# A scan's diagonal blocks moved by GpSimd, and its scale put on the keys

## Chip, cores and metric

The kernel runs on one core of a Trainium2 chip. The metric is the device time of one execution in microseconds. A profile of one execution stands beside the times: it names the engines PE (TensorE matmuls), PEld (TensorE weight loads), DVE (VectorE), ACT (ScalarE), POOL (GpSimd) and SP (SyncE), and writes a q behind the name where only the engine's queue is meant, as in ACTq for a DMA that ScalarE begins.

## The reference

One encoder layer on a 1024 x 1024 input: a normalization, one wide projection, two token mixers (a convolution module, and a bidirectional gated scan with 8 heads of 128), a gated merge, an output product, and a feed-forward block. All in float32. The part that matters here is the scan:

```python
qh = heads(jax.nn.silu(q) * (HGRN_HEAD_DIM ** -0.5))
lf_f, k_f = _forget_log_and_key(z_fwd, lb_fwd)    # f = lb + (1-lb) sigmoid(z)
lf_b, k_b = _forget_log_and_key(z_bwd, lb_bwd)    # key = (1-lb) sigmoid(-z)
o_fwd = _chunk_gated_scan(qh, heads(k_f), vh, heads(lf_f))
o_bwd = flip(_chunk_gated_scan(flip(qh), flip(heads(k_b)), flip(vh), flip(heads(lf_b))))
# S_t = diag(f_t) S_{t-1} + k_t v_t^T,  o_t = S_t^T q_t
...
```

So the key of each direction carries a factor per channel, `1 - lb`, and the query a constant, `128 ** -0.5`. Their product `kscale` (one column per head and direction) may be put on either side of the score `q k`.

## The kernel before

The projection, the merge and the feed-forward block are long rows of float32 products, each split into three products of rounded parts (`mm3`, lines 148 to 150). The scan is woven into the end of the projection. It goes head by head, and each head in two halves of 512 positions, so 16 scans `i`, each with a chain of its own:

- `scan_inputs(i)` loads `q` and the two gates' inputs, and ScalarE makes from each input the key's sigmoid into `kG` (line 1162), the gate's sigmoid (1163) and the forget gate `f` (1164); VectorE clips `f` (1165). `kG` has both directions side by side, 2 x 512 columns, as have `f` and `qF`.
- `scan_base` builds the scores inside blocks of 32 positions by doubling: at each size `h` a copy of the keys and of the queries is woven together on ScalarE (`woven`, line 1175, tiles `A`), VectorE multiplies half of `kG` and of `qF` by the totals of the forget gates (`double_keys`, `double_queries`, `totals`, all shown at line 1143), and TensorE makes small products (`level`, 1194). The result is gathered by masks into `D_t`, 128 x 4 x 32 (lines 1260 and 1262).
- `scan_levels` goes on to 64 and 128, with TensorE making the larger blocks (`blocks`, 1284). ScalarE copies them to `S_t` (1312), 128 x 4 x 128, and four DMAs put the four diagonal blocks of `D_t` into `S_t` (1314), 32 partitions and 16 KB each.
- `scan_states` turns the keys on TensorE (1324), copies them on ScalarE (`kT`, 1326) and forms the states (1333).
- `outputs`, one head later, multiplies `S_t`, `qF` and the states with values (1374), copies the result (`tm`, 1376), squares it (1379), takes the norm on GpSimd (`ors`, 591 and 592), and scales (1393).

The loop over heads and halves runs `scan_levels` and `scan_states` of scan `i`; `between(n)` after each piece puts in some TensorE work of the projection (`dense.fill(FILL)`), one step of the previous head's `outputs`, and one step of `scan_base` of the scans `i + 1` (`ahead`) or `i + 2` (`following`).

TensorE's order is the order in which the program writes its instructions:

```python
ctx.enter_context(tc.manual_schedule(engines={mybir.EngineType.PE}))
```

The other engines' orders are made by a planner from the dependences, a cost model and the order of writing; each engine then runs its queue strictly in that order. Tiles have a fixed number of buffers (8 for `A`, 3 for `kG`, `D` and `S`, 4 for `qF`), and a new one waits until the readers of the oldest are done.

`nc.scalar`, also called `A`, is ScalarE; `V` is VectorE, `G` GpSimd, `T` TensorE. `tt` is a VectorE product of two tensors, `view(t, off, dims)` an access pattern by offset and steps, and `pairs(t, h)` the pattern that takes, in the two directions, every second block of `h` columns.

Of the kernel before, what the change touches and what calls it, by code (L numbers as in the profile page):

```python
# [15 lines left out]
ALU = mybir.AluOpType  # L16
# [15 lines left out]
H = 512  # L32
# [5 lines left out]
def view(t, off, dims):  # L38

    return bass.AP(  # L40
        tensor=t.tensor,
        offset=t.offset + off,
        ap=[list(t.ap[0])] + [list(d) for d in dims],
    )
# [3 lines left out]
def tile_hybrid_encoder(  # L48
# [22 lines left out]
    nc = tc.nc  # L71
    PSUM = bass.MemoryType.PSUM
    V, A, G, T = nc.vector, nc.scalar, nc.gpsimd, nc.tensor
# [20 lines left out]
    def nm(s):  # L94
        uid[0] += 1
        return f"{s}_{uid[0]}"
# [3 lines left out]
    def bank(tag):  # L100
        return ps.tile([P, H], F32, tag=tag, name=nm(tag), bufs=BANKS[tag])

    def page(pool, tag, bufs, dt=F32):
        return pool.tile([P, H], dt, tag=tag, name=nm(tag), bufs=bufs)
# [10 lines left out]
    def load(src):  # L115
        t = tmp()
        nc.sync.dma_start(t, src)
        return t
# [670 lines left out]
    for j in range(NCW):  # L789
        g = gp0.tile([P, PAD + S + PAD], F32, tag="gl", name=nm("gl"), bufs=NCW)  # L790
# [341 lines left out]
    for k in range(NK2):  # L1132
        t = load(d_h[k][1])
# [8 lines left out]
    def tt(o, a, b, op=ALU.mult):  # L1142
        V.tensor_tensor(o, a, b, op=op)  # L1143
# [4 lines left out]
    def c4(t):  # L1148
        return t.rearrange("p (c t) -> p c t", c=4)
# [18 lines left out]
    def pairs(t, h, other=H):  # L1168

        return view(t, 0, [[other + h, 2], [2 * h, H // (2 * h)], [1, h]])  # L1170

    def woven(t, h):

        t_h = page(hp, "A", 8)
        A.copy(pairs(t_h, h, 0), pairs(t, h))  # L1175
        return t_h

    def slot(b, n):
        return b[:, n * P : (n + 1) * P]

    def near(t):
        return t.rearrange("p (c t) -> p c t", c=4)

    def over(m):
        return view(m, 0, [[0, 4], [1, 32]])

    def each():
        for c in range(4):
            for g in range(0, P, 32):
                yield c * P + g, slice(g, g + 32), slice(32 * c, 32 * c + 32)  # L1190

    def level(b, A_t, Q_t):
        for at, g, o in each():
            T.matmul(b[g, o], A_t[:, at : at + 32], Q_t(at), start=True, stop=True)

    def row(t):
        return lambda at: t[:, at : at + 32]

    def double_keys(kG, tb, h):
        n, nb = H // (2 * h), H // h  # L1200
        tt(pairs(kG, h), pairs(kG, h), view(tb, 1, [[nb - 1, 2], [2, n], [0, h]]))

    def double_queries(qF, q, tb, h):
        n, nb = H // (2 * h), H // h
        tt(pairs(qF, h), q, view(tb, nb + 1, [[-(nb + 1), 2], [2, n], [0, h]]))

    def totals(tb, h, to=None):
        n, nb = H // (2 * h), H // h
        tn = None
        if to is None:  # L1210
            tn = hp.tile([P, 2, n], F32, tag=f"tb{h}", name=nm("tb"), bufs=1 if h < 8 else 2)
            to = view(tn, 0, [[n, 2], [1, n]])
        tt(to, view(tb, 0, [[nb, 2], [2, n]]), view(tb, 1, [[nb, 2], [2, n]]))
        return tn

    def scan_base(ins):


        q, f, kG, ks = ins
        qF = hp.tile([P, 2, H], F32, tag="qF", name=nm("qF"), bufs=4)  # L1220
        D_t = hp.tile([P, 4, 32], F32, tag="D", name=nm("D"), bufs=3)
        k_d, Q1 = page(hp, "A", 8), page(hp, "A", 8)
        V.tensor_scalar(k_d, kG[:, 1, :], ks[:, 1:2], None, op0=ALU.mult)
        V.scalar_tensor_tensor(k_d, kG[:, 0, :], ks[:, 0:1], k_d, op0=ALU.mult, op1=ALU.add)
        A1 = woven(kG, 1)
        odd = H // 2

        def gated(to, at, t, d):
            V.scalar_tensor_tensor(
                view(to, at, [[2, odd]]),  # L1230
                view(q, t, [[2, odd]]),
                ks[:, d : d + 1],
                view(f, d * H + t, [[2, odd]]),
                op0=ALU.mult,
                op1=ALU.mult,
            )

        for t in range(2):
            gated(Q1, t, t, 1 - t)
        for t in (1, 0):  # L1240
            gated(qF, (1 - t) * H + t, t, t)
        double_keys(kG, f, 1)
        double_queries(qF, pairs(Q1, 1, 0), f, 1)
        tb = totals(f, 1)
        yield
        A2, Q2 = woven(kG, 2), woven(qF, 2)
        double_keys(kG, tb, 2)
        double_queries(qF, pairs(qF, 2), tb, 2)
        tb = totals(tb, 2)
        A4, Q4 = woven(kG, 4), woven(qF, 4)  # L1250
        yield
        b = bank("sc")
        for n, (k_t, q_t) in enumerate(((k_d, q), (A1, Q1), (A2, Q2), (A4, Q4))):
            level(slot(b, n), k_t, row(q_t))
        double_keys(kG, tb, 4)
        double_queries(qF, pairs(qF, 4), tb, 4)
        tb = totals(tb, 4)
        A8, Q8 = woven(kG, 8), woven(qF, 8)
        yield
        A.copy(D_t, near(slot(b, 3)))  # L1260
        for n, m in enumerate((m_d, m_1, m_2)):
            V.copy_predicated(D_t, over(m), near(slot(b, n)))
        double_keys(kG, tb, 8)
        double_queries(qF, pairs(qF, 8), tb, 8)
        tb = totals(tb, 8)
        A16, Q16 = woven(kG, 16), woven(qF, 16)
        yield
        double_keys(kG, tb, 16)
        double_queries(qF, pairs(qF, 16), tb, 16)
        tb = totals(tb, 16)  # L1270
        yield qF, kG, tb, D_t, A8, Q8, A16, Q16

    def scan_levels(base, S_t, Tt):


        qF, kG, tb, D_t, A8, Q8, A16, Q16 = base

        def blocks(b, h):

            for c in range(0, H, P):  # L1280
                for s0 in range(0, P, h):
                    t0 = s0 ^ h
                    d = s0 // h % 2
                    T.matmul(
                        b[s0 : s0 + h, c + t0 : c + t0 + h],
                        kG[:, d, c + s0 : c + s0 + h],
                        qF[:, 1 - d, c + t0 : c + t0 + h],
                        start=True,
                        stop=True,
                    )  # L1290

        def double(tb, h, to=None):
            double_keys(kG, tb, h)
            double_queries(qF, pairs(qF, h), tb, h)
            return totals(tb, h, to)

        b = bank("ob")
        level(slot(b, 0), A8, row(Q8))
        level(slot(b, 1), A16, row(Q16))
        S_b = bank("sc")  # L1300
        for at, g, _ in each():
            T.matmul(S_b[g, at : at + 32], none, none, start=True, stop=True)
        blocks(S_b, 32)
        for n, m in enumerate((m_8, m_16)):
            V.copy_predicated(D_t, over(m), near(slot(b, n)))
        tb = double(tb, 32)
        yield
        yield
        b = S_b
        blocks(b, 64)  # L1310
        double(tb, 64, view(Tt, 0, [[4, 2], [1, 4]]))
        A.copy(S_t, c4(b))
        for g in range(0, P, 32):
            nc.scalar.dma_start(S_t[g : g + 32, :, g : g + 32], D_t[g : g + 32])
        yield

    def scan_states(i, kG, v, Tt, Sf, Sb):
# [91 lines left out]
    class Base:  # L1409
        def __init__(self, ins):  # L1410
            self.gen, self.val = scan_base(ins), None
# [40 lines left out]
    for h in range(NH):  # L1452
# [4 lines left out]
        for half in range(2):  # L1457
# [11 lines left out]
            S_t = hp.tile([P, 4, P], F32, tag="S", name=nm("S"), bufs=3)  # L1469
# [9 lines left out]
            qF, kG = base[:2]  # L1479
# [499 lines left out]
    for s in range(SEVENS):  # L1979
        todo = [(FIRST + 2 * NS * s, i, k) for i in PRODUCTS for k in range(NS)]  # L1980
        if s == 0:
            at = [12 + 2 * n for n in range(12)] + [starts[0] - 8 + n // 2 for n in range(6)]
            at += [starts[0] - 5 + n for n in range(3)]
        else:
            at = [starts[s] - 36 + 6 * n for n in range(NS)]
# [59 lines left out]
```

## Time and profile before

| | before |
|---|---|
| median of 3 runs | 1735.89 us (1734.44 to 1736.55) |
| the profiled execution | 1732.47 us |
| its span, first to last instruction | 1730.7 us |
| mean granted TensorE clock | 0.998 |
| DMAs begun by GpSimd (software queue) | 44800 packets, 37.76 MB |
| DMAs begun by ScalarE (queue 10) | 9216 packets, 1.05 MB |

Engine times are shares of the span. A busy TensorE is not one at its peak, but TensorE idle is time in which nothing was multiplied. The idle time of an engine ends with what released it; where the text before `<-` is an engine and line, that is the one that waited. In the windows' rows the last columns are the granted TensorE clock as a share of full speed, the mean busy share of the DMA engines and GB/s. The queue of ScalarE carries only the 64 transfers of line 1314; all others are begun by SyncE or GpSimd.

### The profile page before, as it was taken

Reading aid. Unit: us, or ns where it says so; the run is one execution under the profiler, and the core shown is the slowest. Engines: PE = TensorE matmul, PEld = TensorE weight load, DVE = VectorE, ACT = ScalarE, POOL = GpSimd, SP = SyncE. Lnnn points to the kernel's source line nnn. Section 1 sums busy time; section 2 is a strip of 40 time slices with the busy share of each in tenths; the row PEclk is TensorE's granted clock in tenths of the full one; section 3 lists DMA queues with packets and bytes.
Section 4 is the critical chain, followed back from the end, with each engine's and each line's share of the span. In section 5 each row is a group of like instructions: output and inputs, shape, how many; then the busy total and the mean of one; then the engine's idle time right before and its main releaser. Section 6 shows DMA issues by size and latency. Waiting matters only on the chain. (4 is left out here: it accounts for less than half of the span.)

```text
span 1730.7 us, 30713 instructions
## 1 busy us (share of the span) xinstructions
PE 1702.4 (98%) x11902; PEld 1415.8 (82%) x11902; DVE 1257.2 (73%) x1953; ACT 824.4 (48%) x1544; POOL 170.6 (10%) x185
## 2 busy tenths in 40 slices
PE   8999999999999999999999999999999999999997
PEld 6878887888788888888888888888888888888787
DVE  4599999746778888878657466767776877657864
ACT  7444433334566777776442245444434443542334
POOL 2211111100000000000000002011111111000110
PEclk9999999999999999999999999999999999999999
DMA  8768887855673434435579466577777877783842
GB/s 285 241 170 187 197 193 187 210 160 156 207 226 102 133 127 133 127 115 186 176 249 331 153 205 206 145 155 149 174 172 156 183 170 162 231 263 102 213 93 98
DMA packets 343752, 308.28 MB, mean 178 GB/s; under 512 B 25262, under 2 KB 255798, under 8 KB 343606
## 3 DMA queue, kind: packets, MB, share of 16 engines
q1 hardware_dynamic: 289590, 267.51, 48.7%
q0 software_dynamic: 44800, 37.76, 15.2%
q10 hardware_dynamic: 9216, 1.05, 0.4%
q8 instruction: 93, 1.52, 0.3%
q14 instruction: 53, 0.43, 0.1%
HBM read 201.40 MB, written 87.03 MB: 167 GB/s over the span
## 5 line engine op out<-in xcount | busy, mean ns | idle before, releaser
L148 PE MATMUL mm<-hx,wp 128*128 128x512 f32 x1068 | 427.3, 400 | 2.7 <-ACT tm L850 1.5
L150 PE MATMUL mm<-hx,wp 128*128 128x512 f32 x1068 | 417.5, 391 | 1.2 <-DVE wp L124 1.2
L149 PE MATMUL mm<-hx,wp 128*128 128x512 f32 x1068 | 416.6, 390 | 0.0
L124 ACT CAST wp<-wr 128x1024 fp32r<-128x1024 f32 (+2 forms) x147 | 147.3, 1002 | 254.3 <-PE mm L149 111.0
L150 PEld LDWEIGHTS mm<-hx,wp 128*128 128x128 f32 x1068 | 200.6, 188 | 46.2 <-DVE wp L124 3.4
L148 PEld LDWEIGHTS mm<-hx,wp 128*128 128x128 f32 x1068 | 200.9, 188 | 45.4 <-DVE ev L799 2.2
L149 PEld LDWEIGHTS mm<-hx,wp 128*128 128x128 f32 x1068 | 201.0, 188 | 39.8 <-issue 1.0
L124 DVE TENSOR_TENSOR wp<-wr,wp 128x1024 fp32r<-128x1024 f32 (+2 forms) x145 | 169.5, 1170 | 71.2 <-ACT wp L124 64.8
L1038 DVE SCALAR_TENSOR_TENSOR acc<-gl,v_b,acc 128x1024 f32<-128x1024 f32 x120 | 149.1, 1279 | 0.4
L439 ACT COPY su<-mm 128x512 f32<-128x512 f32 x82 | 47.7, 581 | 56.9 <-PE mm L150 56.3
L1143 DVE TENSOR_TENSOR qF<-qF,tb 128x512 f32<-128x512 f32 x96 | 65.7, 686 | 6.9 <-ACT A L1175 6.7
L148 PE MATMUL tr<-hx,wp 128*128 128x512 f32 x180 | 70.5, 392 | 0.0
L124 ACT CAST wq<-sw 128x1024 fp32r<-128x1024 f32 x41 | 43.2, 1054 | 56.8 <-PE mm L149 46.2
L150 PE MATMUL tr<-hx,wp 128*128 128x512 f32 x180 | 70.1, 389 | 0.0
L149 PE MATMUL tr<-hx,wp 128*128 128x512 f32 x180 | 70.0, 389 | 0.0
L1641 DVE SCALAR_TENSOR_TENSOR tm<-gp,v_a,tm 128x512 f32<-128x512 f32 x88 | 66.0, 750 | 3.9 <-ACT tm L1639 2.0
L1143 DVE TENSOR_TENSOR kG<-kG,tb 128x512 f32<-128x512 f32 x96 | 65.1, 685 | 0.5 <-ACT A L1175 0.4
L148 PE MATMUL mm<-hy,wp 128*128 128x512 f32 x164 | 64.2, 391 | 0.0
L148 PE MATMUL sc<-hy,wq 128*128 128x512 f32 x164 | 64.2, 391 | 0.0
L150 PE MATMUL sc<-hy,wq 128*128 128x512 f32 x164 | 63.8, 389 | 0.0
L149 PE MATMUL mm<-hy,wp 128*128 128x512 f32 x164 | 63.8, 389 | 0.0
L149 PE MATMUL sc<-hy,wq 128*128 128x512 f32 x164 | 63.8, 389 | 0.0
(372 smaller groups left out, 3616.5 us busy)
## 6 DMA issues: line engine op xcount, KB each, us to landing
wr<-in_w_in_dram SPq DMA_DIRECT2D x48, 512.0 KB, 4.8
wr<-in_ffn_w_up_dram SPq DMA_DIRECT2D x22, 512.0 KB, 4.0
sw<-in_w_in_dram SPq DMA_DIRECT2D x38, 256.0 KB
d_g<-ft SPq DMA_DIRECT2D x38, 256.0 KB, 2.8
sw<-in_ffn_w_up_dram SPq DMA_DIRECT2D x38, 256.0 KB, 4.5
sw<-in_ffn_w_up_dram POOLq DMA_DIRECT2D x19, 512.0 KB, 8.1
wr<-sw POOLq DMA_DIRECT2D x32, 256.0 KB, 3.4
wr<-wr POOLq DMA_DIRECT2D x32, 256.0 KB, 4.0
```

Source lines behind the costliest of these rows:

```text
L124: parts = A.copy(hi, src), eng.tensor_tensor(lo, src, hi.bitcast(F32), op=ALU.subtract)
L148: T.matmul(acc, whi[:, k, :], ahi, start=first, stop=False, skip_group_check=again)
L149: T.matmul(acc, whi[:, k, :], alo, start=False, stop=False, skip_group_check=again)
L150: T.matmul(acc, wlo[:, k, :], ahi, start=False, stop=last, skip_group_check=again)
L439: A.copy(t, acc)
L1038: V.scalar_tensor_tensor(acc, g[:, k : k + S], tap(k), acc, op0=ALU.mult, op1=ALU.add)
L1143: V.tensor_tensor(o, a, b, op=op)
L1641: V.scalar_tensor_tensor(c, g[:, o + k : o + k + H], vec("fdw", k * NF + j), c, op0=ALU.mult, op1=ALU.add,)
```

## The change

Two places in the scan. In `scan_levels` the four DMAs from `D_t` to `S_t` are begun by GpSimd. In `scan_base` both directions of `kG` are multiplied in place by their column of `kscale`; the sum `k_d` of the directions is then a plain addition, and `Q1` and the first half of `qF` are each one product of `q` and `f` with a pattern over both parities, where there were two products with a scalar for each.

```diff
         D_t = hp.tile([P, 4, 32], F32, tag="D", name=nm("D"), bufs=3)
+        for d in range(2):
+            V.tensor_scalar(kG[:, d, :], kG[:, d, :], ks[:, d : d + 1], None, op0=ALU.mult)
         k_d, Q1 = page(hp, "A", 8), page(hp, "A", 8)
-        V.tensor_scalar(k_d, kG[:, 1, :], ks[:, 1:2], None, op0=ALU.mult)
-        V.scalar_tensor_tensor(k_d, kG[:, 0, :], ks[:, 0:1], k_d, op0=ALU.mult, op1=ALU.add)
+        tt(k_d, kG[:, 0, :], kG[:, 1, :], ALU.add)
         A1 = woven(kG, 1)
         odd = H // 2
-
-        def gated(to, at, t, d):
-            V.scalar_tensor_tensor(
-                view(to, at, [[2, odd]]),
-                view(q, t, [[2, odd]]),
-                ks[:, d : d + 1],
-                view(f, d * H + t, [[2, odd]]),
-                op0=ALU.mult,
-                op1=ALU.mult,
-            )
-
-        for t in range(2):
-            gated(Q1, t, t, 1 - t)
-        for t in (1, 0):
-            gated(qF, (1 - t) * H + t, t, t)
+        tt(
+            pairs(Q1, 1, 0),
+            view(q, 0, [[1, 2], [2, odd], [1, 1]]),
+            view(f, H, [[1 - H, 2], [2, odd], [1, 1]]),
+        )
+        tt(
+            view(qF, 1, [[H - 1, 2], [2, odd]]),
+            view(q, 1, [[-1, 2], [2, odd]]),
+            view(f, H + 1, [[-(H + 1), 2], [2, odd]]),
+        )
         double_keys(kG, f, 1)
...
         A.copy(S_t, c4(b))
         for g in range(0, P, 32):
-            nc.scalar.dma_start(S_t[g : g + 32, :, g : g + 32], D_t[g : g + 32])
+            G.dma_start(S_t[g : g + 32, :, g : g + 32], D_t[g : g + 32])
         yield
```

## The prediction

> **What bounds the kernel now.** I read the page first, then the busy time by windows, then the waits and the timeline inside the stage that the change touches.
>
> ```profile
> span 1730.7 us, 30713 instructions
> PE 1702.4 (98%) x11902; PEld 1415.8 (82%) x11902; DVE 1257.2 (73%) x1953; ACT 824.4 (48%) x1544; POOL 170.6 (10%) x185
> 486.00:880.00 394.00, 386.45 (x5966) 329.88 (x5964) 308.33 (x683) 268.02 (x612) 14.69 (x16) 1.00 0.46 145
> 915.00:1600.00 685.00, 685.00 (x3027) 566.61 (x3026) 464.07 (x638) 279.38 (x411) 73.23 (x69) 1.00 0.70 183
> ```
>
> TensorE is busy 98% of the span. The scan stage runs from 486 to 880 us; the first two lines of the windows give it and the later stage: columns are PE, PEld, DVE, ACT, POOL busy, clock, DMA share, GB/s. In the scan TensorE is busy 386.45 of 394.00, so at most 7.55 us can be won there by waiting less, while from 915 to 1600 it is never idle and nothing can be won. TensorE's order is written out by hand, so its work is the same before and after; only its waits can change. These are they, for the scan stage:
>
> ```profile
> PE tr L1324 <- DVE kG L1143: 4.7, 3, 2.2
> PE sc L1333 <- ACT kT L1326: 1.4, 2, 0.7
> PE sc L1194 <- ACT A L1175: 1.3, 2, 1.0
> ```
>
> So TensorE waits for the finished keys (`kG`) before it turns them, for ScalarE's copy of the turned keys (`kT`), and for ScalarE's weaves (`A`). The longest of these waits is followed by a slower clock:
>
> ```profile
> 720.00:724.00 4.00, 1.86 (x9) 1.87 (x10) 4.00 (x7) 0.88 (x2) 0.00 (x0) 0.74 0.84 258
> 724.00:728.00 4.00, 4.00 (x19) 3.33 (x19) 4.00 (x10) 3.83 (x8) 0.00 (x0) 0.83 0.70 217
> 722.14 1.11 PE L1324 MATMUL tr<-ident,kG 128*128 128x128 f32 x4 [2.24 <-DVE kG L1143]
> ```
>
> The missing clock in the two windows is 0.26 x 4 + 0.17 x 4 = 1.7 us. I put it down to the 2.24 us wait just in front of it. [...]
>
> **The four transfers leave ScalarE.**
>
> ```profile
> L1314 ACTq DMA_DIRECT2D S<-D x64: 592/612/1323, 523.1 to 856.5; - x64
> 676.53 2.55 ACTq L1314 DMA_DIRECT2D S<-D  x4
> 679.18 1.05 ACT L124 CAST wp<-wr 128x1024 fp32r<-128x1024 f32 x1 [2.68 <-DMA S<-D]
> 680.13 0.58 ACT L1326 COPY kT<-tr 128x512 f32<-128x512 f32 x1
> 680.76 0.94 PE L1333 MATMUL sc<-v,kT 128*128 128x128 f32 x6 [0.63 <-ACT kT L1326]
> ```
>
> Each of the 16 scans holds ScalarE's queue for about 2.55 us (four issues of 0.612 and their gaps), 16 x 2.55 = 41 us. Idle time "until DMA S<-D" is this issuing. At 676.53 it stands in front of a cast and of `kT`; `kT` ends at 680.71 and TensorE starts at 680.76, after 0.63 us of waiting. With the four issues gone `kT` can be 2.55 us earlier, so both waits of this kind vanish: -1.4.
>
> The other place is further from TensorE:
>
> ```profile
> 697.83 1.92 ACTq L1314 DMA_DIRECT2D S<-D  x3
> 700.88 0.39 PE L1374 MATMUL ob<-Sf,qF 128*128 128x128 f32 x2
> 702.31 0.59 ACT L1376 COPY tm<-ob 128x512 f32<-128x512 f32 x1
> 706.16 0.20 POOL L591 TENSOR_SCALAR ors<-oss 128x8 f32<-128x8 f32 x1 [43.64 <-ACT jk L1379]
> 712.32 0.70 DVE L1165 TENSOR_SCALAR f<-f 128x1024 f32<-128x1024 f32 x1 [2.67 <-ACT f L1164]
> 714.13 0.69 DVE L1143 TENSOR_TENSOR kG<-kG,tb 128x512 f32<-128x512 f32 x1
> 714.73 0.69 DVE L1143 TENSOR_TENSOR qF<-qF,tb 128x512 f32<-128x512 f32 x1
> 715.33 0.48 DVE L1229 SCALAR_TENSOR_TENSOR qF<-q,kscale,f 128x256 f32<-128x256 f32 x1
> 715.73 0.68 DVE L1143 TENSOR_TENSOR kG<-kG,tb 128x512 f32<-128x512 f32 x1
> 721.39 0.69 DVE L1143 TENSOR_TENSOR kG<-kG,tb 128x512 f32<-128x512 f32 x1
> ```
>
> This chain ends in the 2.24 us wait. The transfers keep ScalarE until 699.75, so the copy `tm` of the finished output starts at 702.31 though the matmuls ended at 701.27: 1.04 us late. After it come squares, GpSimd's `ors` at 706.16, the scaling on ScalarE, the forget gate `f`, VectorE's clip at 712.32, and then VectorE without a pause until `kG` is done at 722.08, 0.06 us ahead of TensorE. Without the issues `tm` starts on time and the chain moves by up to 1.04. I take all of it for this wait, and half of what remains of the other waits for `kG` (4.7 - 2.24 = 2.5, half 1.2) and of those for `A` (1.3, half 0.65), as the same chain lies in front of them with smaller lateness.
>
> **What GpSimd pays.**
>
> ```profile
> L301 POOL DMA_DIRECT2D wr<-wr x32: 847/856/866, 128.6 to 1464.2; - x32
> L301 POOL DMA_DIRECT2D sw<-in_w_in_dram x13: 1570/1582/1757, 85.6 to 327.8; - x13
> DMA to landing us min/median/max: 3.2/4.4/9.8
> 854.53 2.56 ACTq L1314 DMA_DIRECT2D S<-D  x4
> 870.46 0.39 PE L1374 MATMUL ob<-v,S 128*128 128x128 f32 x2
> ```
>
> A transfer begun by GpSimd has 0.86 us for the small and 1.58 for the large form (medians). No such transfer of 16 KB is in the trace; I take the small one, 4 x 0.86 = 3.4 us a scan, bounds 3.4 to 6.3. GpSimd is free: 14.69 of 394 us busy. What stands behind the four on its queue is `ors`: at the quoted head they would begin at 697.2 and end by 703.5 at the dear price, ahead of 706.16. Landing takes 3.2 to 9.8 us from issue. The tightest use of a block seen is the last one: begun at 854.53, last issue at 854.5 + 3 x 1.58 = 859.3, landed at 869.1 at worst, used at 870.46. Cost nothing; it is hidden by the 16 us between copy and use, and if that cover were gone it would cost the overshoot, up to some 8 us at one place (a rival below).
>
> **The scaling moves from queries to keys.**
>
> ```profile
> L1223 DVE TENSOR_SCALAR A<-kG,kscale 128x512 f32<-128x512 f32 x16 | 7.7, 480 | 4.9 <-ACT kG L1162 4.9
> L1224 DVE SCALAR_TENSOR_TENSOR A<-kG,kscale,A 128x512 f32<-128x512 f32 x16 | 12.0, 747 | 0.2
> L1229 DVE SCALAR_TENSOR_TENSOR qF<-q,kscale,f 128x256 f32<-128x256 f32 x32 | 14.7, 481 | 3.4 <-PE ob L1374 3.3
> L1229 DVE SCALAR_TENSOR_TENSOR A<-q,kscale,f 128x256 f32<-128x256 f32 x32 | 14.4, 481 | 0.0
> L1143 DVE TENSOR_TENSOR qF<-A,f 128x512 f32<-128x512 f32 x16 | 11.0, 688 | 0.0
> ```
>
> Removed per scan: 480 + 747 + 4 x 481 = 3151 ns. Added: two scalings of 480 and three products of 688 (nearest row: `qF<-A,f`, same size and stride), 3024 ns. By durations VectorE gains 0.13 us a scan, 2 us over 16, not on the path as a sum. What matters is where. Back to back, instructions start closer than they last: 0.60 apart for the product (714.13 to 714.73), 0.40 for the half-size one (715.33 to 715.73). In the unbroken run to 722.08 stand the two half-size `qF` instructions, 0.80 together; one product of 0.60 replaces them: -0.19 on the long wait. The two scalings (0.40 each by the same overlap, an estimate) need only the key's sigmoids, which ScalarE makes before `f`; VectorE idles 2.67 us in front of 712.32, and I place them there, at no cost. If that cover is gone they cost 0.80 a scan. The wait that is added: the first weave of a scan on ScalarE reads `kG` and now waits for both scalings, with the weaves, casts and evacuations of its queue behind it, and VectorE's first `kG` product waits for that weave. Bounds: 0 (the Q1 and qF products, 1.2 us, lie between) and the price of the slower rival. I take 0.
>
> **Sum.** -1.4 (kT) -1.04 -0.19 (long wait) -1.2 -0.65 (other waits) = -4.5; with the long wait at about 1.0 in place of 2.24 the clock stays up, -1.7: -6.2. The profiled execution took 1732.47 us (span 1730.7 and 1.8 around it), 3.4 below the median of the runs, 1735.89, and 2.0 below their lowest, so the difference is carried over: 1735.9 - 6.2 = 1729.7.
>
> **Rivals.**
>
> *Slower: the scaled keys become a link VectorE to ScalarE to VectorE.*
>
> ```profile
> ACT A L1175 <- DVE kG L1143: 17.7, 23, 2.5
> ```
>
> ScalarE's waits for keys cost 17.7 / 23 = 0.77 us each. If the first weave joins them in every scan, and in half of the scans (one of each head, where an unbroken VectorE run ends in the turn of the keys) the delay passes through, TensorE waits 8 x 0.77 = 6.2 more; two more waits that pull the clock down add 3.4; the sure -1.4 stays: +8.2, 1744.1. It decides from 0.06 us, the distance between `kG` and TensorE at 722.08. For it: this slack, and that VectorE, ScalarE and GpSimd are ordered by a planner, so new dependences reshuffle all three. Against it: the idle 2.67.
>
> *No change: the freed queue time is spent waiting.* ScalarE would then wait for the matmuls of `ob` or for GpSimd's `ors`; only the -1.4 remains: 1734.5.
>
> *GpSimd and VectorE hinder each other.* 64 x 0.86 = 55 us of GpSimd issuing is 14% of the stage; of 48 VectorE scalings and clips 6.7 would meet one, at up to 0.86 each: +5.8, which eats the gain: 1735.5. The trace has no such meeting of these shapes. [...]
>
> *The transfers go late.* If the planner puts `ors` in front of the four, or they land at the slow end behind it, the last block misses 870.46 by up to 8 us while only -6.2 is won: about 1738.
>
> **How the numbers follow.** About 0.2%, 3.5 us, is what a measurement of this kernel can tell from no change. Forecast 0.40; no change 0.13 and hindrance 0.06 make "same" 0.19; slower by the link 0.33, late transfers 0.04, another shuffle of the order 0.04 make 0.41. The forecast's own range runs from all waits and the clock (-7.55 - 1.7, 1726.6) to the edge of the bound (1732.4). The whole range reaches from there over no change to the slower rival, 1726.6 to 1744.5, and leaves worse shuffles out.
>
> **What would show it.** Right: no transfer on ScalarE's queue and no wait "until DMA S<-D"; no TensorE wait for `kT`; waits for `kG` near 2 us in sum and full clock at all windows; TensorE idle below 3 us in the scan stage. Wrong: clip or scalings standing at the end of long VectorE idle times, first weaves waiting for the scalings, more or longer waits for `kG`, further windows with clock below 1, transfers of GpSimd far over 1 us each, or TensorE waiting for `S`.

## The result, and the profile after

The changed kernel took 1729.89 us (median of 9 runs, 1728.12 to 1733.97) beside 1734.67 us for the kernel before on the same chip: a ratio of 0.9971 [0.9961, 0.9981], that is 3.3 to 6.8 us less. The forecast was 1729.7.

From the profile's page of the changed kernel (its head and the busy times):

```profile
span 1732.2 us, 30782 instructions
...
PE 1704.5 (98%) x11902; PEld 1416.5 (82%) x11902; DVE 1255.2 (72%) x1937; ACT 826.1 (48%) x1544; POOL 206.5 (12%) x249
```

This profiled execution, 1733.97 us, is the slowest of the nine, and its span is no shorter than the one before. So whole spans can't be subtracted; the stage has to be compared by itself. Two rows of each profile mark it: the first product of the first scan (`sc<-q,A`, first start) and the last product of the outputs (`ob<-v,S`, last start). Before:

```profile
L1194 PE MATMUL sc<-q,A x512: 196/196/218, 503.0 to 831.7; 128*32 128x32 f32 x171
L1374 PE MATMUL ob<-v,S x128: 272/275/275, 558.0 to 872.6; 128*128 128x128 f32 x128
```

After:

```profile
L1194 PE MATMUL sc<-q,A x512: 196/196/218, 504.7 to 825.9; 128*32 128x32 f32 x171
L1370 PE MATMUL ob<-v,S x128: 272/275/275, 559.5 to 866.8; 128*128 128x128 f32 x128
```

The stage took 872.6 - 503.0 = 369.6 before and 866.8 - 504.7 = 362.1 after. 1.7 of the 7.5 is the low clock that lay inside the stage before; about 6 is left. After, the windows' row of the stage (columns as before) with the rows at two low clocks outside it, and then the waits of TensorE and VectorE in the stage:

```profile
486.00:880.00 394.00, 390.16 (x5999) 334.55 (x5998) 311.07 (x671) 271.48 (x618) 50.36 (x80) 1.00 0.47 149
...
96.00:100.00 4.00, 2.11 (x5) 1.72 (x6) 2.31 (x4) 2.16 (x4) 0.00 (x0) 0.69 0.98 313
900.00:904.00 4.00, 2.95 (x9) 1.88 (x10) 3.15 (x6) 1.96 (x4) 0.00 (x0) 0.89 1.07 314
```

```profile
PE tr L1320 <- DVE kG L1143: 3.8, 3, 2.0
...
DVE kG L1223 <- ACT kG L1162: 25.3, 13, 4.6
...
DVE f L1165 <- ACT f L1164: 6.1, 6, 1.4
DVE qF L1143 <- ACT A L1175: 4.6, 7, 2.0
```

Of VectorE's waits before, the prediction did not show these:

```profile
DVE f L1165 <- ACT f L1164: 17.9, 8, 5.5
...
DVE qF L1143 <- ACT A L1175: 6.7, 11, 2.3
```

TensorE is idle for 3.84 us instead of 7.55. Its waits for `kT` and for `A` are gone; those for `kG` are left. VectorE's idle time stands in front of the keys' scalings (L1223), where the prediction put them: 25.3 us there and 6.1 in front of the clip, where it had 17.9. ScalarE has no wait "until DMA S<-D" any more. The timeline at the two places that the prediction followed:

```profile
676.77 0.59 ACT L1308 COPY S<-sc 128x512 f32<-128x512 f32 x1
677.28 1.05 ACT L124 CAST wp<-wr 128x1024 fp32r<-128x1024 f32 x1
...
677.66 2.25 POOL L1310 DMA_DIRECT2D S<-D  x4 [13.42 <-ACT S L1308]
...
678.73 0.58 ACT L1322 COPY kT<-tr 128x512 f32<-128x512 f32 x1
...
709.86 0.49 DVE L1223 TENSOR_SCALAR kG<-kG,kscale 128x512 f32<-128x512 f32 x1 [3.46 <-ACT kG L1162]
...
711.86 0.69 DVE L1165 TENSOR_SCALAR f<-f 128x1024 f32<-128x1024 f32 x1 [0.96 <-ACT f L1164]
...
721.56 0.66 PE L1320 MATMUL tr<-ident,kG 128*128 128x128 f32 x4 [1.38 <-DVE kG L1143]
```

Behind the copy to `S` ScalarE goes straight on to the cast and `kT`, while GpSimd issues the four transfers beside it. One scaling ends a VectorE wait of 3.46 us, and the wait at `kG` is 1.38.

### The profile page after: what moved, and what is told of

The parts are those of the page before. It is cut to its first block, busy times and chain, and to the rows that moved or that the text cites. A ratio compares the mean times of both kernels' runs of the same rounds, so it can differ in the third digit from the quotient of the medians.

```text
span 1732.2 us, 30782 instructions
## 1 busy us (share of the span) xinstructions
PE 1704.5 (98%) x11902; PEld 1416.5 (82%) x11902; DVE 1255.2 (72%) x1937; ACT 826.1 (48%) x1544; POOL 206.5 (12%) x249
## 5 line engine op out<-in xcount | busy, mean ns | idle before, releaser
L1310 POOL DMA_DIRECT2D S<-D x64 | 35.5, 560 | 286.7 <-ACT jk L1375 127.7
L148 PE MATMUL sc<-hy,wq 128*128 128x512 f32 x164 | 64.2, 391 | 0.0
L150 PE MATMUL sc<-hy,wq 128*128 128x512 f32 x164 | 63.8, 389 | 0.0
```

What stands on the lines that cost most here:

```text
L148: T.matmul(acc, whi[:, k, :], ahi, start=first, stop=False, skip_group_check=again)
L150: T.matmul(acc, wlo[:, k, :], ahi, start=False, stop=last, skip_group_check=again)
L1310: G.dma_start(S_t[g : g + 32, :, g : g + 32], D_t[g : g + 32])
```

## The experiments

The theory: ScalarE's queue time was what TensorE waited behind, and the keys' scalings cost nothing, since they stand in VectorE's idle time. The rivals: the scaled keys are a link that delays ScalarE and VectorE; GpSimd's issuing hinders VectorE; the low clock explains the difference; the planner's new order is only a lucky one.

**The transfers alone, to GpSimd.** The kernel before with

```diff
-            nc.scalar.dma_start(S_t[g : g + 32, :, g : g + 32], D_t[g : g + 32])
+            G.dma_start(S_t[g : g + 32, :, g : g + 32], D_t[g : g + 32])
```

> The kernel before with one edit: the four transfers begun by GpSimd; the queries are scaled as before. Theory A (the gain comes from ScalarE's freed queue): 0.6 to 0.85 of the change, -3 to -4.5 us, no TensorE wait for kT, TensorE idle in the scan stage down from 7.55 to about 4. Theory B (the gain comes from VectorE's work moved into its idle times): at most -1.4 us, the two waits for kT. Theory C (the gain is a lucky order of the planner's): anything, with no relation to the sum of the parts.

1732.5 beside 1736.4: 0.998 [0.9968, 0.9992]. TensorE's waits in the stage:

```profile
PE tr L1324 <- DVE kG L1143: 4.4, 5, 1.7
PE sc L1194 <- ACT A L1175: 0.8, 1, 0.8
```

The waits for `kT` are gone with this part alone. A wait of 0.8 for a weave is left, and the waits for `kG` are shorter but more.

**The keys alone.** The change without that line: ScalarE goes on issuing the transfers.

> The kernel before with the other edit: keys scaled twice by VectorE, transfers begun by ScalarE as before. Theory A: -0.2 to -1.2 us (0.19 a run of VectorE, six runs), waits for kT still 1.4 us. Theory B: -3.5 to -5 us. Theory C: anything; e1 and e2 together far from the -5.0 of the whole change.

1738.03 beside 1736.4: 1.0008 [0.9998, 1.0018], no gain. The waits of TensorE and VectorE in the stage:

```profile
PE tr L1320 <- DVE kG L1143: 4.8, 3, 2.2
PE sc L1194 <- ACT A L1175: 1.9, 2, 1.5
PE sc L1329 <- ACT kT L1322: 1.4, 2, 0.9
...
DVE kG L1223 <- ACT kG L1162: 27.0, 14, 4.0
...
DVE qF L1143 <- ACT A L1175: 9.2, 13, 2.3
```

VectorE waits in front of the scalings as in the changed kernel, but waits longer for ScalarE's weaves (9.2 us; 6.7 before, 4.6 after), and TensorE's three kinds of waits are those of before. Its low clock stands behind the wait at 588, not at 722 (windows):

```profile
588.00:592.00 4.00, 3.61 (x14) 3.12 (x15) 4.00 (x10) 1.92 (x5) 0.00 (x0) 0.64 0.65 171
592.00:596.00 4.00, 4.00 (x26) 3.51 (x25) 2.76 (x10) 3.86 (x8) 0.00 (x0) 0.94 0.38 115
```

**The transfers alone, to SyncE.** As the first, with `nc.sync.dma_start`: no GpSimd instruction is added.

> The kernel before with the four transfers begun by SyncE. Theory A (what counts is that they leave ScalarE): as with GpSimd, within 1 us of e1. Rival D (GpSimd's queue was needed, since SyncE's is full of loads behind waits): the transfers hold up the loads of the scans and of the weights behind them, 0 to +5 us against the kernel before, with new waits for loads (q, zi, wr) in the scan stage.

1730.91 beside 1736.4: 0.9967 [0.9956, 0.9979]. Its waits are those of GpSimd's version (`kG` 4.5 in 5, `A` 0.8 in 1), and its stage is 364.6 beside 364.8. So what counts is that ScalarE is left, not who takes over.

**The keys scaled by ScalarE.** The change without VectorE's two scalings; ScalarE makes the key, scale included, as an affine function of the gate's sigmoid:

```diff
             A.activation(kG[:, d, :], z, AF.Sigmoid, scale=-1.0)
...
+            A.activation(
+                kG[:, d, :], z, AF.Identity,
+                scale=knegative[:, ks : ks + 1], bias=kscale[:, ks : ks + 1],
+            )
...
-        for d in range(2):
-            V.tensor_scalar(kG[:, d, :], kG[:, d, :], ks[:, d : d + 1], None, op0=ALU.mult)
```

> The changed kernel with the scaling of the keys done by ScalarE in the gate itself: the key is kscale - kscale x sigmoid(z), one instruction of about 0.82 us in place of a sigmoid of 0.63, and VectorE's 32 scalings of 0.48 are gone. Theory A: VectorE's scalings stood in idle time, so taking them away wins under 0.5 us; ScalarE's longer key instruction (2 x 0.19 a scan) lies in front of the clip and costs up to 0.2 to 0.4 us at each of the waits for kG: 0 to +1.5 us against the changed kernel. Theory E (the link from VectorE's scalings to the first weaves costs time): -1 to -2.5 us against the changed kernel.

1732.05 beside 1736.4: 0.9979 [0.9968, 0.999]. Here there is no link from VectorE's scaling to ScalarE's first weave, and VectorE has the 32 scalings less in the scan. TensorE's waits:

```profile
PE tr L1324 <- DVE kG L1143: 3.0, 4, 1.4
```

The stage is 362.3, that of the changed kernel. The link has no price that shows in the stage. (ScalarE's instruction for the key has the form of the one that makes `f` here, 816 ns beside 632 for the key's sigmoid in the first trace of the kernel before, so that this run by itself could hide a small price; the last experiment doubles the scalings instead.)

**The change with the transfers on SyncE.**

> The changed kernel with the four transfers begun by SyncE in place of GpSimd: scaled keys and a free ScalarE, GpSimd left out. Theory A (it counts that ScalarE is free; then the scaled keys are worth 1.5 to 2.7 us more): 1.0 us about the changed kernel, -5 to -7.5 us against the kernel before, scan stage from first to last of its products about 362 us. Rival D (SyncE's loads are held up when the scan runs faster): slower than the changed kernel by 1 us or more, with new waits for loads. Rival F (GpSimd's issuing hinders VectorE in the changed kernel): faster than the changed kernel by 2 us or more.

1729.65 beside 1736.81: 0.9955 [0.9941, 0.9969]; stage 363.5, of which 1.7 is a low clock from 588.7 on.

**Twice the issues on GpSimd.** The change with eight transfers of 16 partitions in place of four of 32:

```diff
-        for g in range(0, P, 32):
-            G.dma_start(S_t[g : g + 32, :, g : g + 32], D_t[g : g + 32])
+        for g in range(0, P, 16):
+            o = g // 32 * 32
+            G.dma_start(S_t[g : g + 16, :, o : o + 32], D_t[g : g + 16])
```

> The changed kernel with each transfer cut in two, 8 by GpSimd a scan in place of 4: the suspected cost on GpSimd is doubled (2.2 us more a scan at the 0.55 us that one was seen to take). Theory A (hidden in the 14 us and more between copy and use): within 1 us of the changed kernel. Rival F (GpSimd's issuing locks VectorE out): VectorE's scalings and clips beside an issue last longer than 0.50 and 0.70 us, and the time is 1 to 5 us over the changed kernel. Rival G (the norm behind the transfers on GpSimd's queue is late): TensorE waits for kG grow by 1 us or more.

1729.83 beside 1736.81: 0.9956 [0.9942, 0.9971]. The rows of the transfers' line, and that of VectorE's scalings among the instructions on `kG`:

```profile
L1311 POOL DMA_DIRECT2D S<-D x128: 512/512/767, 524.4 to 852.6; - x128
...
DMA to landing us min/median/max: 1.6/2.7/4.8
```

```profile
L1223 DVE TENSOR_SCALAR kG<-kG,kscale x32: 469/486/494, 491.0 to 797.0; 128x512 f32<-128x512 f32 x32
```

The scalings last 469 to 494 ns. Few of them overlap an issue: four here, at 475 to 478 ns, and none in the changed kernel. With the transfers alone, however, nine of the 16 scalings of this size do, at 472 to 480 ns, beside 476 to 487 for the other seven. No scaling is held up for the length of an issue, and the rival of a hindrance falls for them; no clip (L1165) overlaps an issue in these three traces, so clips stay untested. The stage is 362.7: TensorE has one wait of 0.6 us that the change has not, for which the profile names no cause.

**The kernel before again,** one execution, for the spread of its trace.

> The kernel before, unchanged, once more with a profile: how far do the waits and the clock of one profile hold? Theory A of the prediction (the 2.24 us wait at 722 us halves the clock behind it): the same wait and the same low clock behind it. [...]

1735.43 us. The wait that the prediction made answerable for the low clock is there again; the low clock is not. Timeline and windows:

```profile
723.41 0.66 PE L1324 MATMUL tr<-ident,kG 128*128 128x128 f32 x4 [2.22 <-DVE kG L1143]
...
817.04 0.39 PE L150 MATMUL mm<-hx,wp 128*128 128x512 f32 x1
818.53 1.16 PE L1333 MATMUL sc<-v,kT 128*128 128x128 f32 x8 [1.10 <-ACT kT L1326]
```

```profile
96.00:100.00 4.00, 2.85 (x8) 2.28 (x9) 1.90 (x4) 2.20 (x4) 0.15 (x1) 0.71 0.76 238
...
720.00:724.00 4.00, 1.78 (x13) 1.37 (x12) 4.00 (x7) 2.15 (x5) 0.00 (x0) 1.00 0.55 175
724.00:728.00 4.00, 4.00 (x26) 3.49 (x25) 4.00 (x10) 2.56 (x5) 0.00 (x0) 1.00 1.01 298
```

**Both: keys by ScalarE, transfers by SyncE.** VectorE and GpSimd are spared.

> The kernel with the key's scale put in by ScalarE's gate instruction (no scaling on VectorE) and the transfers begun by SyncE. Theory A: as the version with GpSimd and that scaling within 1 us, -3 to -5 us against the kernel before, since VectorE's scalings stood in idle time. Theory E (the link from VectorE's scalings to the first weaves costs time): faster than the version of scaled keys and SyncE by 1 us or more.

1731.74 beside 1736.81: 0.9965 [0.9953, 0.9978]; stage 362.0. Sparing either engine brings nothing beyond the change.

**A product moved to GpSimd.** In front of the waits that are left VectorE runs without a pause, so the changed kernel (transfers on SyncE) was tried with the projection's weight subtraction (`wp`, 1.22 us on VectorE) on GpSimd:

```diff
-    rest_jobs = [std_job(in_cols(c), ND, h_std, e) for c, e in rest[:-2]]
+    rest_jobs = [std_job(in_cols(c), ND, h_std, e, eng=G) for c, e in rest[:-2]]
```

> Scaled keys, transfers by SyncE, and the subtraction that splits the projection's weights taken from VectorE to GpSimd in the scan stage (17 of 1.22 us; two of them stand in the VectorE runs that end in the long waits for kG). Theory A (the remaining waits of 2.0, 0.4 and 1.4 us are VectorE's unbroken runs after the clip): the two long waits shorten by up to 1.2 us each, -1.5 to -2.5 us against the changed kernel. Rival: GpSimd takes about twice as long for the same subtraction and the weights come late, so that TensorE waits for wp: 0 to +5 us.

1739.24 beside 1737.46: 1.0016 [1.0007, 1.0025], slower by a little. TensorE's waits for `kG` grow to 9.3 us; the waits, the timeline in front of the wait of 3.0 at 592, VectorE's instructions on `qF`, and the window of that wait:

```profile
PE tr L1320 <- DVE kG L1143: 9.3, 4, 3.2
```

```profile
583.64 2.70 POOL L124 TENSOR_TENSOR wp<-wr,wp 128x1024 fp32r<-128x1024 f32 x1 [6.71 <-ACT wp L124]
...
584.00 2.89 DVE L1143 TENSOR_TENSOR qF<-q,f 128x512 f32<-128x512 f32 x1
```

```profile
L1143 DVE TENSOR_TENSOR qF<-qF,tb x96: 674/683/2782, 503.1 to 856.1; 128x512 f32<-128x512 f32 x96
```

```profile
588.00:592.00 4.00, 1.23 (x8) 0.82 (x6) 3.96 (x8) 2.36 (x6) 0.00 (x0) 1.00 0.92 288
```

VectorE's product begins 0.36 us after GpSimd's and ends 0.55 us behind it: 2.89 us instead of 0.69. In the last row TensorE is busy 1.23 of 4 us, and its clock is 1.00.

**The change again,** beside the kernel that follows and the one above.

> The changed kernel, unchanged, beside the others on the same chip and with a second profile: -4 to -6 us against the kernel before; the scan stage from first to last of its products within 1 us of 362.1, the waits for kG 3.8 in sum.

1731.82 beside 1737.46: 0.9976 [0.9964, 0.9988]. Its profiled execution took 1726.87 us (span 1725.0), 7.1 less than the first one's, with the same stage, 362.1, and the same waits (`kG` 3.8 in 3). The 7.1 lie outside the scan; 3.4 of them are the two low clocks at 96 and 900, which this trace has not.

**The scalings twice.** The change with a second pass, by 1.0, behind each:

```diff
             V.tensor_scalar(kG[:, d, :], kG[:, d, :], ks[:, d : d + 1], None, op0=ALU.mult)
+            V.tensor_scalar(kG[:, d, :], kG[:, d, :], 1.0, None, op0=ALU.mult)
```

> The changed kernel with a second scaling, by 1.0, behind each scaling of the keys: 32 more VectorE instructions of 0.48 us (0.40 apart, 0.8 us a scan). Theory A (the scalings stand in VectorE's idle time before the clip): under 1 us over the changed kernel. The prediction's slower rival (the scaled keys are a link from VectorE to ScalarE to VectorE in front of the weaves): 0.8 us at each of the six to eight odd scans, +4 to +6 us, less where a scan has slack.

1733.82 beside 1737.46: 0.9978 [0.9967, 0.9988], like the change in the same batch. The stage is 364.0, of which 1.7 is a low clock at 589.5. Another 32 instructions of some 0.48 us left the stage where it was.

All of them together, stage by the two marking rows, TensorE's idle time as 394 less its busy time in the windows' row of 486 to 880:

| kernel | stage, us | low clock in it | without it | TensorE idle |
|---|---|---|---|---|
| before, first and second trace | 369.6, 368.4 | 1.7, 0 | 367.9, 368.4 | 7.6, 8.1 |
| keys alone | 369.4 | 1.7 | 367.7 | 8.0 |
| transfers alone, GpSimd / SyncE | 364.8 / 364.6 | 0 | 364.8 / 364.6 | 5.4 / 5.3 |
| the change, first and second trace | 362.1, 362.1 | 0 | 362.1 | 3.8, 3.8 |
| ... transfers on SyncE | 363.5 | 1.7 | 361.8 | 3.7 |
| ... eight transfers | 362.7 | 0 | 362.7 | 4.3 |
| ... scaled twice | 364.0 | 1.7 | 362.3 | 4.0 |
| ... keys by ScalarE, GpSimd / SyncE | 362.3 / 362.0 | 0 | 362.3 / 362.0 | 3.1 / 3.1 |
| ... product on GpSimd | 370.5 | 0 | 370.5 | 11.3 |

From the mean of the two traces before, 368.1, the transfers are worth 3.4 of the 6.0, the keys 2.6 on top of them, and at most 0.7 by themselves.

## Why the prediction was right, point by point

TensorE's 5856 recorded products between the two marks come in the same order in all traces, so each distance from start to start can be set beside its fellow. Between the second trace of the kernel before, which has no low clock in the stage, and the changed kernel, these distances give the 6.2 us: 2.8 at the states behind `kT`, 2.0 at the products behind the weaves `A`, 1.1 at the turns behind `kG`, 0.3 over the rest.

**The transfers leave ScalarE: right, and under-sized.** The term was -1.4, measured 2.8; some 0.3 of the difference is that the two waits for `kT` are longer in the second trace (1.7 us in sum) than in the first (1.4). The rest lies in how a wait is counted. A recorded wait begins where the product in front of it is taken to end. That was not what the wait cost. In the second trace of before, quoted above, the states started 818.53 - 817.04 = 1.49 us after the last product; in the changed kernel

```profile
812.41 0.39 PE L150 MATMUL mm<-hx,wp 128*128 128x512 f32 x1
812.64 1.05 PE L1329 MATMUL sc<-v,kT 128*128 128x128 f32 x8
```

it is 0.23: 1.26 won where 1.10 was recorded as a wait. A product of this row is recorded as 0.39 us long, though the next one can start 0.23 behind its start: each wait hides 0.39 - 0.23 = 0.16, and shorter delays don't appear as waits.

**The waits for `A`: right, and under-sized.** Half of 1.3 was taken; all were won, 2.0 by the distances.

**The long wait for `kG`: right in its chain, over-sized.** -1.23 was forecast; it went from 2.24 and 2.22 to 1.38, by 0.85. The chain moved as forecast. In the changed kernel the last product of `ob` in front of it, the copy `tm` and the last product of the keys are

```profile
701.39 0.39 PE L1370 MATMUL ob<-Sf,qF 128*128 128x128 f32 x2
...
701.82 0.59 ACT L1372 COPY tm<-ob 128x512 f32<-128x512 f32 x1 [1.34 <-PE ob L1370]
...
720.82 0.69 DVE L1143 TENSOR_TENSOR kG<-kG,tb 128x512 f32<-128x512 f32 x1
```

so `tm` starts 0.04 us behind `ob` instead of 1.04, and from the end of `ob` to the clip it takes 10.08 us instead of 11.05: 0.97 won. VectorE's run from the clip to the last product of the keys takes 9.65 instead of 9.76, 0.11 won where 0.19 was forecast. But TensorE, with fewer delays of its own, is at the turn of the keys 0.23 sooner behind `ob` (18.40 us instead of 18.63). The forecast left that out: 0.97 + 0.11 - 0.23 = 0.85.

**The other waits for `kG`: failed.** Half of 2.5, 1.2, was to go. The waits at 769 and 814 went (0.3 and 0.9 by the distances), but those at 589 and 634 grew by 0.3 and 0.6, so 0.3 is left. The step that failed is "the same chain lies in front of them with smaller lateness": the chain is there, but its lateness did not leave with the transfers. The timeline of the changed kernel has, in front of the longest remaining wait,

```profile
569.13 0.71 ACT L1175 COPY A<-kG 128x512 f32<-128x512 f32 x1 [1.56 <-DVE kG L1143]
...
569.72 0.61 ACT L1372 COPY tm<-ob 128x512 f32<-128x512 f32 x1
...
577.79 0.49 DVE L1223 TENSOR_SCALAR kG<-kG,kscale 128x512 f32<-128x512 f32 x1 [3.51 <-ACT kG L1162]
...
579.60 0.69 DVE L1165 TENSOR_SCALAR f<-f 128x1024 f32<-128x1024 f32 x1 [0.77 <-ACT f L1164]
...
582.62 1.22 DVE L124 TENSOR_TENSOR wp<-wr,wp 128x1024 fp32r<-128x1024 f32 x1
...
589.83 0.66 PE L1320 MATMUL tr<-ident,kG 128*128 128x128 f32 x4 [2.03 <-DVE kG L1143]
```

ScalarE now has a weave of the next scan's keys ahead of `tm`, and waits 1.56 us for VectorE there. So `tm` starts 0.3 us behind the end of `ob`, as late as before. In front of the wait at 634 the same kind of weave waits 2.00 us, and `tm` is 0.31 late instead of 0.04. At these places the freed queue time is spent waiting, which the rival "no change" had for the whole kernel, though for other releasers. From 579.60 on VectorE has work of its own, the projection's subtraction among it: 10.17 us to the last product of the keys, 9.91 before. With the keys on ScalarE this wait was 1.36 and the one at 721 gone, but others came at 680 and 767 (0.4 and 0.8): the order that the planner finds moves the waits about. Why it puts the weave there was not tested.

**The clock: failed.** The 1.7 was put down to the 2.24 us wait in front of it. The same wait of 2.22 in the second trace has clock 1.00 behind it, and the low clock stands in 96 to 100. The changed kernel has it there and at 900 to 904. In all traces 11 waits of 1.97 us or more stand in the stage; behind four of them, of 1.97 to 2.24 us, the clock fell (in the first trace of the kernel before to 0.50 from 722 to 725), and behind seven, the two longest (3.0 and 3.2, product on GpSimd) among them, it did not. So a wait of this length alone does not account for a low clock, and the change can't be credited with 1.7. What else decides it, no run here shows.

So -4.5 + -1.7 came to the right sum by two errors against each other: the clock's 1.7 wasn't there, and the waits were worth 6.2, not 4.5. That the time itself came within 0.2 us of 1729.7 is luck as well: the measured gain is 4.8, not 6.2, from a kernel before that took 1734.67 here and not 1735.89, and 5.6 beside the later executions.

**The scalings at no cost: right.** Doubled, or taken off VectorE, they left the stage where it was, and in the changed kernel's trace no instruction is recorded as waiting for one. The keys' gain comes from what the change takes out behind them. With the transfers alone VectorE takes 2.04 us from the first instruction of the keys' sum to the first product of the keys (565.06 to 567.10), in the changed kernel 1.40 (567.01 to 568.41): about 0.45 less for the sum, now one addition, and 0.2 less for `Q1`. The weave ahead of `tm` waits for that product. With the transfers alone it is

```profile
567.82 0.70 ACT L1175 COPY A<-kG 128x512 f32<-128x512 f32 x1 [2.22 <-DVE kG L1143]
```

where the changed kernel waits 1.56 us. At four outputs (near 569, 613, 657 and 790 us) `tm` is 0.96 to 1.03 us late with the transfers alone, and 0.31 to 0.46 in the changed kernel. Neither in the kernel before nor with the keys alone does ScalarE wait for such a weave just ahead of these copies. That fits a gain that needs the transfers away from ScalarE, which the stages show (at most 0.7 alone, 2.6 on top). How much of the 2.6 comes by this way is not worked out, and no run changes the sum or the queries' products by themselves.

**GpSimd's price: right in what it hides, too dear.** 0.552 us an issue instead of 0.86 and landing in 1.6 to 4.9 us instead of 3.2 to 9.8:

```profile
L1310 POOL DMA_DIRECT2D S<-D x64: 552/552/634, 525.0 to 850.7; - x64
DMA to landing us min/median/max: 1.6/2.6/4.9
```

No engine waits for `S`.

**The rivals.** The slower link falls: without it the stage is the same, though ScalarE does wait longer for keys (21.3 us in 20 waits instead of 17.7 in 23), all of it for products of line 1143 and none for a scaling. Its condition, 0.06 us from the end of `kG` to TensorE, was no margin: TensorE was waiting for `kG` there, and had no wait for `A` left. "No change" falls by the stage, late transfers by the last line quoted, and hindrance by the scalings that overlap an issue. A lucky order is unlikely: scaled twice, or with the keys on ScalarE, VectorE's order differs from the changed kernel's in 100 to 160 of some 640 places of the stage, the scalings among them, and all six versions of the change without the moved product take 361.8 to 362.7 us, low clock left out. Of what would show the forecast right, three signs failed: 3.84 us of idle TensorE instead of under 3, waits for `kG` of 3.8 instead of near 2, and a clock below 1 at 96 and 900. Of what would show it wrong, two signs came true and cost the stage nothing: scalings stand at the end of long VectorE idle times, 25.3 us in 13, and the windows at 96 and 900 are further ones with a low clock.

By times alone the parts can't be told apart: the transfers alone (0.998 [0.9968, 0.9992], SyncE 0.9967 [0.9956, 0.9979]) overlap the change. That the keys add 2.6 rests on the stages of the traces. No version was clearly better than the changed kernel.

## What to carry to other kernels

Where an engine's queue carries casts and copies that TensorE waits for, DMA issues between them held that queue here for their full time (2.55 us a scan, 41 in all), though only what reached TensorE was won (3.4 us of stage). Begin them on a queue that has no such copies, and look for what moves up into the freed time: here it was a weave that waits for VectorE. Price a TensorE wait by the distance from start to start, against a place where nothing is late, rather than by the recorded idle time. Take a low clock in one trace for a property of the kernel only when a second trace shows it at the same place.

## What the runs showed of the hardware

- A product of two tensors on VectorE (0.69 us) took up to 2.89 us beside a GpSimd subtraction (2.5 us on the mean of 15) in the trace with the product on GpSimd. Two clips, which read one tensor, took 2.29 us instead of 0.69 in the same way. Of the ten products and clips of the stage that were lengthened, eight ended 0.55 us behind the subtraction.
- For GpSimd's DMA issues, of which the prediction feared the like, no such lengthening was seen: with 128 of them the scalings stayed at 469 to 494 ns. Where a scaling began 0.04 to 0.18 us behind an issue, the issue was the longer one: 639 and 732 ns with the transfers alone and 767 with eight of them, where the other issues beside a scaling took 512 to 564.
- A low clock of some 1.7 us in sum is not tied to a place in the program: it stood behind the wait at 722, behind that at 588, near 97 or near 903, in traces whose TensorE order is the same.
